# Output projection of a hybrid decoder layer by pairs of column blocks, part of it in seven products

## The chip, the cores and the metric

One core of a Trainium2 chip runs the whole layer in one program. The metric is the device time of one execution in microseconds (us). TensorE (PE in the profile) multiplies, VectorE (DVE) and ScalarE (ACT) do the elementwise work, GpSimd (POOL) and SyncE (SP) mostly issue transfers.

## The reference

Batch 1, 256 tokens, width 2048, everything in float32. The part that matters:

```python
mixed = sigmoid(g_a) * y_a + sigmoid(g_b) * y_b          # (256, 2048); y_a: gated DeltaNet, y_b: pooling mixer
x = x + einsum('bsd,de->bse', mixed, w_out)              # the output projection, w_out (2048, 2048)
h = rmsnorm(x, norm_ffn_w)
gate, up = split(einsum('bsd,df->bsf', h, w_up), 2)      # the up projection, w_up (2048, 11264)
```

`g_a` is the last of the input products (`w_in`, 2048 x 14368) that are made for each of four groups of 512 features (four heads).

## The kernel before, in words

*Numbers.* Each float32 operand is split into a high part (rounded to the reduced format of the fast matmul) and a low part (the rest), and a product is the sum of three matmuls: high by high, low by high, high by low. A weight tile is 256 rows by 512 columns, held as 128 partitions x 2 x 512. ScalarE makes its high part (`whi`, line 317), VectorE its low part (`wlo`, line 328). There are three buffers of each, and `weights()` asks for the split of the tile two ahead (`AHEAD`). Raw tiles come over SP's queue in the order of the list `srcs`, into four buffers (`load_part`, line 223).

*A product.* `gemm_a` makes 256 tokens x 512 columns: for each weight tile, two blocks of 128 features, two halves of the tokens, three matmuls (lines 365 to 367), so twelve matmuls of 128x512. After each six it calls `side()`, which advances a generator of other work by one step.

*The order of groups.* For g = 0 to 3 the input products go k, q, v, p, g_b, z and g_a (eight tiles each, and two of the pooling weights). The delta rule `gdn(g, ...)` is such a generator. For g = 3 its last part runs behind: it waits until `ending` is set, which is done before the last two tiles of the g_a product, and its matmuls (lines 1011 to 1078) are put between those of g_a and of the output projection, one step for each `side()`. The order on TensorE is there fixed as written (`fixed_order`); elsewhere a planner orders every engine by a model of the time, earlier instructions of the program first. After the generator come `gated` (lines 1211, 1215) and, four steps later, `mixed`, which transposes the last group's result and writes its halves `mhi[3]`, `mlo[3]` (lines 1229, 1230).

*The output projection.* Column blocks c = 0 to 3 of 512. Since `mhi[3]` comes late, `early` first makes the tiles 0 to 5 of blocks 0 and 1, with the generator beside them (24 calls of `side()`); then `drain()` ends what is left of it, the mixer's memory pool is closed and that of the feed-forward part (`fp`) is opened in its place. Then tiles 6 and 7 of blocks 0 and 1, and blocks 2 and 3 whole. After each block VectorE adds it to the residual `xts[c]` (line 1270; x came over POOL's queue, line 1258), ScalarE squares it (line 1277), and TensorE transposes it, ScalarE and VectorE scaling and splitting the four rows (lines 1288, 1294, 1295) into `fhl`, the input of the up projection.

*Seven products.* The up projection and the down projection are in part made by the Strassen-Winograd form: two blocks of features by two halves of tokens, and two by two weight tiles (`b11, b12, b21, b22`), need seven products of 256 features by 128 tokens by 512 columns, six matmuls each (`high_first`), in place of eight. Their weights are `b11`, `b21`, `b22` ("11", "21", "22") and four sums T1 to T4, which VectorE makes in place (`up_sum`, line 244) from the loaded quarters (`quad_load`, line 237). T3 and T4 are made from T2 and T2 from T1. The sums of the inputs are made by `four_sums`. In the up projection these products stand between full tiles. A bank is copied (ScalarE) after product 11 and two sums (VectorE, lines 1433 and 1454) are put into other banks before 21 and after T3.

Of the kernel before, what the change touches and what calls it, by code (L numbers as in the profile page):

```python
# [35 lines left out]
def kernel(  # L36
# [40 lines left out]
    def cols(w, base, nk):  # L77
        return [w[c * 256 : (c + 1) * 256, base : base + 512].rearrange("(k p) f -> p k f", p=P)
                for c in range(nk // 2)]

    srcs = []
    for g in range(4):
        for base in (C_K, C_Q, C_V, C_P, C_GB):
            srcs += cols(w_in[0], base + 512 * g, KD)
            if g == 0 and base == C_K:
                srcs += [w_in[0, c * 1024 : (c + 1) * 1024, C_B : C_B + P].rearrange("(k p) f -> p k f", p=P)
                         for c in range(2)]
        parts = [cols(pool_w[0, g], 0, 4), cols(w_in[0], C_Z + 512 * g, KD)]
        for part in parts if g == 3 else parts[::-1]:
            srcs += part  # L90
        srcs += cols(w_in[0], C_GA + 512 * g, KD)
    outw = [cols(w_out[0], 512 * c, KD) for c in range(4)]

    srcs += outw[0][:6] + outw[1][:6] + outw[0][6:] + outw[1][6:] + outw[2] + outw[3]
    NUP = DFF // 512
    TWO = (1, 2, 3, 4, 5, 6, 7, 9)
    chunks_of = [()] + [(1, 0) if c in TWO else (0,) for c in range(1, NUP)]
    UP_PARTS = ("T1", "11", "T2", "21", "T3", "22", "T4")
    up_w = [(cols(w_up[0], 512 * c, KD), cols(w_up[0], DFF + 512 * c, KD)) for c in range(NUP)]
    up_steps = []  # L100
    TAIL = 3
    for c in range(NUP):
# [129 lines left out]
    def quad_load(c, n):  # L232

        ch, i = n // 4, (1, 0, 3, 2)[n % 4]
        up_quarters[c, ch, i] = fp.tile([P, 2, 512], F32, tag=UP_HOMES[1 - c % 2][ch][i], name=nm("quad"))
        with tc.issue_after(last_load[0]):
            last_load[0] = nc.sync.dma_start(up_quarters[c, ch, i], up_w[c][i % 2][2 * ch + i // 2]).ins

    def up_sum(c, what, ch):
        b11, b12, b21, b22 = (up_quarters.get((c, ch, i)) for i in range(4))  # L240
# [53 lines left out]
    def begin(n):  # L294
        while len(made) < min(len(srcs), n):
            load(len(made) + 1)
            raw = loads[len(made)]
            if isinstance(raw, tuple):
                raw, plus, minus = raw
                nc.vector.tensor_tensor(raw, plus, minus, op=ALU.subtract)  # L300
            src = srcs[len(made)]
            shape = list(raw.shape)
            keep = kept.get(len(made))
            behind_conv = ExitStack()
            for ins in last_conv.values():
# [11 lines left out]
            last_cast[0] = nc.scalar.copy(hi, raw).ins  # L317
            if shape[1] == 8:
                lo = None
                nc.vector.tensor_tensor(hi[:, :, 32:64], raw[:, :, 0:32], hi[:, :, 0:32].bitcast(F32),  # L320
                                        op=ALU.subtract)
            else:
                if fourth:
                    lo = fp.tile(shape, F32R, tag="s", name=nm("wlo"))
                else:
                    lo = wpool.tile(shape, F32R, tag="wlo", name=nm("wlo")) if keep is None else \
                        mtile(4 + keep, shape, F32R, nm("klo"))
                last_split[0] = nc.vector.tensor_tensor(lo, raw, hi.bitcast(F32), op=ALU.subtract).ins  # L328
# [3 lines left out]
            made.append((hi, lo))  # L332
            for more in sums_behind.get(len(made) - 1, ()):
# [19 lines left out]

    def gemm_a(lh, ll, nk, steps=None, ps=None):

        ps = pm() if ps is None else ps
        for c in range(nk // 2) if steps is None else steps:
            if c == 1:
                while later:
                    later.pop(0)()  # L360
# [1 line left out]
            for kk in range(2):  # L362
                k = 2 * c + kk
                for t in range(2):
                    mm(ps[:, t, :], lh(k, t), hi[:, kk, :], start=(k == 0), stop=False)  # L365
                    mm(ps[:, t, :], ll(k, t), hi[:, kk, :], start=False, stop=False)  # L366
                    mm(ps[:, t, :], lh(k, t), lo[:, kk, :], start=False, stop=(k == nk - 1))  # L367
                side()
        return ps

    banks = [0]

# [487 lines left out]
    def gdn(g, kq, vt, conv, res):  # L860
# [231 lines left out]
        yield  # L1092
        res.append((po, ro))

    for g in range(4):
        kq = mp.tile([P, 4, 2, S], F32, tag="kq", bufs=1, name=nm("kq"))
        for kind, dst in ((1, kq[:, :, 0, :]), (0, kq[:, :, 1, :])):
            ps = ps_k0 if kind == 1 and g == 0 else gemm_a(xh, xl, KD)
            e = evict(ps)
            convs.append(conv_silu(e, kind, g, dst))  # L1100
            if g:
                later.append(lambda conv=convs[-1]: sum(1 for _ in conv))
            elif kind:
# [152 lines left out]
    def residual(c):  # L1256
        cs = slice(c * 512, (c + 1) * 512)
        return nc.gpsimd.dma_start(xts[c], x[0, :, cs].rearrange("(t p) d -> p t d", p=P)).ins

    residual(0)  # L1260
    residual(1)
    fhl = features("fhl")
    ssq4 = cpool.tile([P, 2, 4], F32, tag="ssq4", name="ssq4b")
    for c in range(4):
        if c < 2:
            ps = gemm_a(at(mhi), at(mlo), KD, range(6, 8), early[c])
        else:
            ps = gemm_a(at(mhi), at(mlo), KD)
        xs = xts[c]
        nc.vector.tensor_tensor(xs, xs, ps, op=ALU.add)  # L1270
        written = nc.gpsimd.dma_start(xt_d[:, :, c * 512 : (c + 1) * 512], xs).ins
# [38 lines left out]
    def four_sums(a11, a12, a21, a22, hi, lo):  # L1310

        s = fp.tile([P, 4, S], F32, tag="s", name=nm("sums"))
        s1, s2, s3, s4 = (s[:, n].rearrange("p (k s) -> p k s", k=2) for n in range(4))
        nc.vector.tensor_tensor(s1, a21, a22, op=ALU.add)
        nc.vector.tensor_tensor(s2, s1, a11, op=ALU.subtract)
        nc.vector.tensor_tensor(s3, a11, a21, op=ALU.subtract)
        nc.vector.tensor_tensor(s4, a12, s2, op=ALU.subtract)
# [4 lines left out]
    def by_halves(h):  # L1322
        return [h[:, 2 * j : 2 * j + 2, t * P : (t + 1) * P] for t in range(2) for j in range(2)]

    y_d = {c: dpool.tile([P, 4, S], F32, tag=f"y{c}", bufs=1, name=f"y{c}") for c in (7, 8, 9)}

# [81 lines left out]

    def fl(k, t):
        return both(fhl, k)[:, 1, t * P : (t + 1) * P]  # L1410

    def high_first(uses, w, first=False):

        for n in range(2):
            for kk in range(2):
                for ps, high, low in uses:
                    for lhs in (high, low) if n == 0 else (high,):
                        mm(ps, lhs(kk), w[n][:, kk], start=(first and n == 0 and kk == 0 and lhs is high), stop=False,  # L1418
                           skip_group_check=True)

    def up_product(c, what, ch):

# [315 lines left out]
```

## Time and profile before

| | |
|---|---|
| median of three runs | 1537.29 us (1536.48 to 1538.0) |
| span of the profiled execution | 1536.8 us |
| TensorE busy | 1524.3 us (99%) |
| VectorE busy | 1268.3 us (83%) |
| ScalarE busy | 853.1 us (56%) |
| split of a weight tile on VectorE (line 328, raw tiles) | 418 times, 1220 ns |
| cast of a weight tile on ScalarE (line 317, raw tiles) | 420 times, 1052 ns |
| output projection on TensorE | from 719.43 us to the last of its products at 818.9 us |

The profiled execution's span agrees with the median of the runs to 0.5 us. A busy share is the time in which the engine has an instruction in flight; matmuls overlap, so the time of a stretch is read from the starts of its instructions. A row of the timeline has start and duration in us, engine, line, operation, output<-inputs, shape and count, and in brackets the idle time before it with what ended it. Rows with a count of more than one are merged.

### The profile page before, as it was taken

How to read it: one execution, taken by the hardware profiler on the slowest of the kernel's cores; microseconds unless marked ns; L12 is line 12 of the kernel's file. 1: busy time of each engine (PE TensorE's matmuls, PEld its weight loads, DVE VectorE, ACT ScalarE, POOL GpSimd, SP SyncE). 2: the span in 40 equal slices, each digit the busy share in tenths (PEclk: the TensorE clock that was granted, in tenths of full speed). 3: DMA queues.
4: the chain of work that ended last, by engine and by line, in shares of the span. 5: the costliest groups of instructions: out<-in, count | busy, mean ns of one | idle time of the engine just before them, and what ended most of it. 6: DMA issues, size and time to landing. Idle time of an engine off the chain costs nothing. (4 is left out here: it accounts for less than half of the span.)

```text
span 1536.8 us, 20233 instructions
## 1 busy us (share of the span) xinstructions
PE 1524.3 (99%) x7290; PEld 1255.4 (82%) x7290; DVE 1268.3 (83%) x1793; ACT 853.1 (56%) x1070; POOL 80.9 (5%) x105
## 2 busy tenths in 40 slices
PE   9999999999999999999999999999999999999997
PEld 8887888787878888788888888788888888888876
DVE  6788859896589858887567899999999886889896
ACT  6455446454455445454455666666666665555553
POOL 1010002000100000000000000000000011010200
PEclk9999999999999999999999999999999999999999
DMA  8776757776576766776588556656457478566662
GB/s 276 209 229 198 203 165 207 218 216 185 148 250 201 208 169 194 231 195 186 171 263 305 179 178 219 219 206 206 154 165 243 127 238 266 172 223 207 235 201 98
DMA packets 166515, 313.62 MB, mean 204 GB/s; under 512 B 19554, under 2 KB 23426, under 8 KB 166286
## 3 DMA queue, kind: packets, MB, share of 16 engines
q1 hardware_dynamic: 157280, 283.17, 59.2%
q0 software_dynamic: 7344, 27.27, 5.5%
q10 hardware_dynamic: 1790, 1.89, 0.4%
q8 instruction: 57, 0.93, 0.3%
q14 instruction: 44, 0.36, 0.1%
HBM read 303.33 MB, written 8.95 MB: 203 GB/s over the span
## 5 line engine op out<-in xcount | busy, mean ns | idle before, releaser
L317 ACT CAST whi<-raw 128x1024 fp32r<-128x1024 f32 x420 | 441.2, 1052 | 427.1 <-PE psm L366 270.0
L328 DVE TENSOR_TENSOR wlo<-raw,whi 128x1024 fp32r<-128x1024 f32 x418 | 507.7, 1220 | 146.0 <-ACT whi L317 140.2
L317 ACT CAST whi<-quad 128x1024 fp32r<-128x1024 f32 x182 | 190.5, 1053 | 136.8 <-PE psg L1418 43.5
L328 DVE TENSOR_TENSOR wlo<-quad,whi 128x1024 fp32r<-128x1024 f32 x182 | 220.0, 1219 | 30.0 <-ACT whi L317 29.4
L367 PE MATMUL psm<-wlo,xhl 128*128 128x512 f32 x432 | 169.5, 393 | 1.3 <-DVE wlo L328 1.2
L365 PE MATMUL psm<-whi,xhl 128*128 128x512 f32 x432 | 169.0, 391 | 0.0
L366 PE MATMUL psm<-whi,xhl 128*128 128x512 f32 x432 | 168.6, 390 | 0.0
L1418 PE MATMUL psg<-whi,fhl 128*128 128x512 f32 x504 | 127.2, 390 | 0.0
L1418 PEld LDWEIGHTS psg<-whi,fhl 128*128 128x128 f32 x504 | 94.5, 188 | 19.6
L367 PEld LDWEIGHTS psm<-wlo,xhl 128*128 128x128 f32 x432 | 81.1, 188 | 18.8 <-DVE wlo L328 2.2
L366 PEld LDWEIGHTS psm<-whi,xhl 128*128 128x128 f32 x432 | 81.1, 188 | 16.8
L365 PEld LDWEIGHTS psm<-whi,xhl 128*128 128x128 f32 x432 | 81.1, 188 | 16.7
L244 DVE TENSOR_TENSOR quad<-quad,quad 128x1024 f32<-128x1024 f32 x72 | 87.6, 1216 | 0.0
L1418 PE MATMUL psg<-wlo,fhl 128*128 128x512 f32 x252 | 69.9, 389 | 0.0
L1418 PE MATMUL psg<-whi,ups 128*128 128x512 f32 x216 | 58.9, 394 | 0.0
L1418 PEld LDWEIGHTS psg<-wlo,fhl 128*128 128x128 f32 x252 | 47.3, 188 | 9.9
L1403 PE MATMUL psm<-whi,hhi 128*128 128x512 f32 (+1 forms) x140 | 54.5, 389 | 0.1
L1403 PE MATMUL psm<-whi,hlo 128*128 128x512 f32 (+1 forms) x140 | 54.1, 386 | 0.0
L1403 PE MATMUL psm<-wlo,hhi 128*128 128x512 f32 (+1 forms) x140 | 54.0, 387 | 0.0
L365 PE MATMUL psm<-whi,mhi 128*128 128x512 f32 x128 | 50.8, 397 | 0.0
L367 PE MATMUL psm<-wlo,mhi 128*128 128x512 f32 x128 | 50.0, 390 | 0.0
L366 PE MATMUL psm<-whi,mlo 128*128 128x512 f32 x128 | 49.9, 390 | 0.0
(435 smaller groups left out, 2953.7 us busy)
## 6 DMA issues: line engine op xcount, KB each, us to landing
raw<-in_w_in_dram SPq DMA_DIRECT2D x224, 512.0 KB, 4.3
raw<-in_w_up_dram SPq DMA_DIRECT2D x104, 512.0 KB, 4.8
quad<-in_w_up_dram SPq DMA_DIRECT2D x72, 512.0 KB, 5.0
raw<-in_w_down_dram SPq DMA_DIRECT2D x56, 512.0 KB, 5.1
raw<-in_w_out_dram SPq DMA_DIRECT2D x32, 512.0 KB, 4.2
quad<-in_w_down_dram POOLq DMA_DIRECT2D x32, 512.0 KB, 5.3
mv<-vrow SPq DMA_DIRECT2D x12, 512.0 KB, 4.8
taps<-in_conv_qkv_w_dram SPq DMA_DIRECT2D x16, 256.0 KB, 6.6
```

What stands on the lines that cost most here:

```text
L244: nc.vector.tensor_tensor(out_, plus_, minus_, op=ALU.subtract)
L317: last_cast[0] = nc.scalar.copy(hi, raw).ins
L328: last_split[0] = nc.vector.tensor_tensor(lo, raw, hi.bitcast(F32), op=ALU.subtract).ins
L365: mm(ps[:, t, :], lh(k, t), hi[:, kk, :], start=(k == 0), stop=False)
L366: mm(ps[:, t, :], ll(k, t), hi[:, kk, :], start=False, stop=False)
L367: mm(ps[:, t, :], lh(k, t), lo[:, kk, :], start=False, stop=(k == nk - 1))
L1403: mm(ps[:, cs], lhs(kk), part_[:, kk, cs], start=(first and kk == 0 and n == 0), stop=(last and kk == 1 and n == 2), skip_group_check=shared)
L1418: mm(ps, lhs(kk), w[n][:, kk], start=(first and n == 0 and kk == 0 and lhs is high), stop=False, skip_group_check=True)
```

## The change

The output projection is made by pairs of column blocks (0 and 1, then 2 and 3). For the first four feature blocks (tiles 0 and 1 of each column block of the pair, which need only `mhi[0]`, `mlo[0]`) the eight products of the two by two form become seven (`pair_product`), one after the other, with no full tile between them; their results lie in the banks in which the remaining tiles (2 to 7) are then added by `gemm_a`. In the first pair `side()` is called after products 1, 3, 5 and 6 (counted from 0), and then after each six matmuls of the tiles 2 to 5 of both blocks. The sums of the input (`out_sums`) are made during the value product of group 3 and split into `osum` during the last g_a product. So that `osum` has a place (the memory of the last four feature blocks of the input), the g_a product of group 3 takes the feature blocks in another order (`GA_LAST`). The quarters of the weights go to memory that other tiles have left (`out_home`), the last two of the second pair to the feed-forward pool.

```diff
+    GA_LAST = (6, 7, 0, 1, 2, 3, 4, 5)
-        srcs += cols(w_in[0], C_GA + 512 * g, KD)
+        ga = cols(w_in[0], C_GA + 512 * g, KD)
+        srcs += ga if g < 3 else [ga[c] for c in GA_LAST]
-    srcs += outw[0][:6] + outw[1][:6] + outw[0][6:] + outw[1][6:] + outw[2] + outw[3]
+    out_pairs = [("out", p) for p in range(2)]
+    srcs += [("up", out_pairs[0], what, 0) for what in UP_PARTS] + outw[0][2:6] + outw[1][2:6]
+    srcs += outw[0][6:] + outw[1][6:]
+    srcs += [("up", out_pairs[1], what, 0) for what in UP_PARTS] + outw[2][2:] + outw[3][2:]
...
+    quads_behind = {}
+    for pair in out_pairs:
+        n = first_part(pair)
+        sums_behind[n - 1] = [(pair, "T1", 0)]
+        for i in range(4 if pair == out_pairs[0] else 2):
+            quads_behind.setdefault(n - 6 + i, []).append((pair, i))
...
+    def out_home(pair, i):
+        if pair == out_pairs[0]:
+            if i < 2:
+                if not halves_kq:
+                    halves_kq.append(mp.tile([P, 2, 2, 512], F32, tag="kq", bufs=1, name=nm("quads")))
+                return halves_kq[0][:, i]
+            return mp.tile([P, 2, 512], F32, tag=("ev", "crow")[i - 2], name=nm("quad"),
+                           **(dict(bufs=1) if i == 2 else {}))
+        if i < 2:
+            return big.tile([P, 2, 512], F32, tag=("x2a", "x2b")[i], name=nm("quad"))
+        return fp.tile([P, 2, 512], F32, tag=("hhi4", "hlo4")[i - 2], name=nm("quad"))
...
+    def pair_product(bank, what, tokens, sums):
+        a, b = bank["ps"]
+        if what in ("11", "21", "T4"):
+            j, t = {"11": (0, 0), "21": (1, 0), "T4": (1, 1)}[what]
+            high, low = (lambda kk, f=f: f(2 * j + kk, t) for f in tokens)
+        else:
+            n = {"T1": 0, "T2": 1, "T3": 2, "22": 3}[what]
+            high, low = (lambda kk, s=s: s[:, n, kk * P : (kk + 1) * P] for s in sums)
+        if what == "21":
+            nc.vector.tensor_tensor(b[:, 0], a[:, 1], bank["own"], op=ALU.add)
+        w = weights()
+        ps = {"T1": a[:, 0], "21": a[:, 0], "22": b[:, 0]}.get(what, a[:, 1])
+        high_first([(ps, high, low)], w, what in ("T1", "11"))
+        if what == "T1":
+            bank["own"] = cpool.tile([P, 512], F32, tag="sqj", name=nm("own"))
+            nc.scalar.copy(bank["own"], a[:, 0])
+        elif what == "11":
+            nc.scalar.copy(a[:, 0], a[:, 1])
+        elif what == "T3":
+            nc.vector.tensor_tensor(b[:, 1], a[:, 1], bank["own"], op=ALU.add)
...
+    def out_sums():
+        h = mp.tile([P, 4, S], F32, tag="mv", name=nm("whole"))
+        nc.vector.tensor_tensor(h, mhi[0].bitcast(F32), mlo[0].bitcast(F32), op=ALU.add)
+        out_s.append(mp.tile([P, 4, S], F32, tag="pu", name=nm("sums")))
+        sums_into(out_s[0], *by_halves(h))
...
-            ps = gemm_a(xh, xl, KD, range(6))
+            ps = gemm_a(xh, xl, KD, GA_LAST[:6])
             ending.append(True)
-            ps = gemm_a(xh, xl, KD, range(6, 8), ps)
+            osum = big.tile([P, 2, 4, S], F32R, tag="x3", name="osum")
+            nc.scalar.copy(osum[:, 0], out_s[0])
+            with tc.issue_after(last_split[0]):
+                nc.vector.tensor_tensor(osum[:, 1], out_s[0], osum[:, 0].bitcast(F32), op=ALU.subtract)
+            ps = gemm_a(xh, xl, KD, GA_LAST[6:], ps)
...
-    early = [gemm_a(at(mhi), at(mlo), KD, range(n)) for n in (6, 6)]
+    def out_pair(sides=()):
+        bank = {"ps": (pm(), pm())}
+        pair = out_pairs[1 if made_pairs else 0]
+        made_pairs.append(bank["ps"])
+        for n, what in enumerate(UP_PARTS):
+            pair_product(bank, what, (at(mhi), at(mlo)), (osum[:, 0], osum[:, 1]))
+            if n in sides:
+                side()
+        return bank["ps"]
+
+    made_pairs = []
+    early = [gemm_a(at(mhi), at(mlo), KD, range(2, 6), ps) for ps in out_pair((1, 3, 5, 6))]
     drain()
...
+    for i in (2, 3):
+        quad_load(out_pairs[1], i)
     residual(0)
...
-            ps = gemm_a(at(mhi), at(mlo), KD)
+            if c == 2:
+                early += out_pair()
+            ps = gemm_a(at(mhi), at(mlo), KD, range(2, 8), early[c])
```

`UP_PARTS` is ("T1", "11", "T2", "21", "T3", "22", "T4"), the order of the seven products. `sums_into` holds the four sums that `four_sums` made in place; `high_first` and `by_halves` are moved up unchanged.

More of the change, by code (lines that the diff above doesn't have):

```diff
@@ L79, in cols @@
                 for c in range(nk // 2)]
+    GA_LAST = (6, 7, 0, 1, 2, 3, 4, 5)
+    UP_PARTS = ("T1", "11", "T2", "21", "T3", "22", "T4")
     srcs = []
@@ L97 @@
     chunks_of = [()] + [(1, 0) if c in TWO else (0,) for c in range(1, NUP)]
-    UP_PARTS = ("T1", "11", "T2", "21", "T3", "22", "T4")
-    up_w = [(cols(w_up[0], 512 * c, KD), cols(w_up[0], DFF + 512 * c, KD)) for c in range(NUP)]
+    up_w = {c: (cols(w_up[0], 512 * c, KD), cols(w_up[0], DFF + 512 * c, KD)) for c in range(NUP)}
+    up_w |= {pair: outw[2 * p : 2 * p + 2] for p, pair in enumerate(out_pairs)}
     up_steps = []
@@ L234, in quad_load @@
         ch, i = n // 4, (1, 0, 3, 2)[n % 4]
-        up_quarters[c, ch, i] = fp.tile([P, 2, 512], F32, tag=UP_HOMES[1 - c % 2][ch][i], name=nm("quad"))
+        if c in out_pairs:
+            home = out_home(c, i)
+        else:
+            home = fp.tile([P, 2, 512], F32, tag=UP_HOMES[1 - c % 2][ch][i], name=nm("quad"))
+        up_quarters[c, ch, i] = home
         with tc.issue_after(last_load[0]):
             last_load[0] = nc.sync.dma_start(up_quarters[c, ch, i], up_w[c][i % 2][2 * ch + i // 2]).ins
+    halves_kq = []
+    def out_home(pair, i):
[9 more added lines that the diff above has]
+        return fp.tile([P, 2, 512], F32, tag=("hhi4", "hlo4")[i - 2], name=nm("quad"))
     def up_sum(c, what, ch):
@@ L332, in begin @@
             made.append((hi, lo))
+            for more in quads_behind.get(len(made) - 1, ()):
+                quad_load(*more)
             for more in sums_behind.get(len(made) - 1, ()):
@@ L354, in gemm_a @@
     def gemm_a(lh, ll, nk, steps=None, ps=None):
+        steps = range(nk // 2) if steps is None else steps
+        first = 2 * steps[0] if ps is None else None
+        last = nk - 1 if ps is not None else 2 * steps[-1] + 1
+        seeded = dict(skip_group_check=ps is not None)
         ps = pm() if ps is None else ps
-        for c in range(nk // 2) if steps is None else steps:
+        for c in steps:
             if c == 1:
@@ L364, in gemm_a, with high_first @@
                 for t in range(2):
-                    mm(ps[:, t, :], lh(k, t), hi[:, kk, :], start=(k == 0), stop=False)
-                    mm(ps[:, t, :], ll(k, t), hi[:, kk, :], start=False, stop=False)
-                    mm(ps[:, t, :], lh(k, t), lo[:, kk, :], start=False, stop=(k == nk - 1))
+                    mm(ps[:, t, :], lh(k, t), hi[:, kk, :], start=(k == first), stop=False, **seeded)
+                    mm(ps[:, t, :], ll(k, t), hi[:, kk, :], start=False, stop=False, **seeded)
+                    mm(ps[:, t, :], lh(k, t), lo[:, kk, :], start=False, stop=(k == last), **seeded)
                 side()
         return ps
+    def pair_product(bank, what, tokens, sums):
[3 more added lines that the diff above has]
+            high, low = (lambda kk, f=f: f(2 * j + kk, t) for f in tokens)
+        else:
+            n = {"T1": 0, "T2": 1, "T3": 2, "22": 3}[what]
[12 more added lines that the diff above has]
+            nc.vector.tensor_tensor(b[:, 1], a[:, 1], bank["own"], op=ALU.add)
+    def high_first(uses, w, first=False):
+        for n in range(2):
+            for kk in range(2):
+                for ps, high, low in uses:
+                    for lhs in (high, low) if n == 0 else (high,):
+                        mm(ps, lhs(kk), w[n][:, kk], start=(first and n == 0 and kk == 0 and lhs is high), stop=False,
+                           skip_group_check=True)
     banks = [0]
@@ L1093, in gdn, with by_halves, sums_into @@
         res.append((po, ro))
+    def by_halves(h):
+        return [h[:, 2 * j : 2 * j + 2, t * P : (t + 1) * P] for t in range(2) for j in range(2)]
+    def sums_into(s, a11, a12, a21, a22):
+        s1, s2, s3, s4 = (s[:, n].rearrange("p (k s) -> p k s", k=2) for n in range(4))
+        nc.vector.tensor_tensor(s1, a21, a22, op=ALU.add)
+        nc.vector.tensor_tensor(s2, s1, a11, op=ALU.subtract)
+        nc.vector.tensor_tensor(s3, a11, a21, op=ALU.subtract)
+        nc.vector.tensor_tensor(s4, a12, s2, op=ALU.subtract)
+    out_s = []
+    def out_sums():
[3 more added lines that the diff above has]
+        sums_into(out_s[0], *by_halves(h))
     for g in range(4):
@@ L1100 @@
             convs.append(conv_silu(e, kind, g, dst))
+            if g == 3 and kind == 0:
+                later.append(out_sums)
             if g:
@@ L1312, in four_sums @@
         s = fp.tile([P, 4, S], F32, tag="s", name=nm("sums"))
[L1313 to L1317, printed above, removed]
+        sums_into(s, a11, a12, a21, a22)
         nc.scalar.copy(hi, s)
@@ L1320, in four_sums @@
         return hi, lo
-    def by_halves(h):
-        return [h[:, 2 * j : 2 * j + 2, t * P : (t + 1) * P] for t in range(2) for j in range(2)]
     y_d = {c: dpool.tile([P, 4, S], F32, tag=f"y{c}", bufs=1, name=f"y{c}") for c in (7, 8, 9)}
@@ L1410, in fl @@
         return both(fhl, k)[:, 1, t * P : (t + 1) * P]
[L1412 to L1419, printed above, removed]
     def up_product(c, what, ch):
```

## The prediction

> **What bounds the kernel now.** I read the page first, then the waits of TensorE, then the timeline of TensorE and VectorE around the output projection (us from the span's start).
>
> ```profile
> span 1536.8 us, 20233 instructions
> PE 1524.3 (99%) x7290; PEld 1255.4 (82%) x7290; DVE 1268.3 (83%) x1793; ACT 853.1 (56%) x1070; POOL 80.9 (5%) x105
> ...
> PE psm L367 <- DVE wlo L328: 1.5, 2, 1.2
> ```
>
> TensorE (PE) works all the time; its longest wait for a weight split adds up to 1.5 us. So the time is TensorE's instruction stream, and a change helps by what it removes from that stream and hurts by each wait it puts in. What is one matmul worth?
>
> ```profile
> 702.04 0.39 PE L365 MATMUL psm<-whi,xhl1a 128*128 128x512 f32 x1
> ...
> 704.76 0.39 PE L365 MATMUL psm<-whi,xhl1b 128*128 128x512 f32 x1
> ```
>
> Twelve matmuls, those of one weight tile, start between these two rows: 2.72 us a tile, 0.227 us a matmul. The 0.39 us in the duration column overlaps the next one and is no price. Beside it the VectorE (DVE), which splits each weight tile into a high and a low half and, in the seven-product form, makes the weight sums:
>
> ```profile
> 863.22 1.22 DVE L244 TENSOR_TENSOR quad<-quad,quad 128x1024 f32<-128x1024 f32 x1
> 864.36 1.22 DVE L328 TENSOR_TENSOR wlo<-quad,whi 128x1024 fp32r<-128x1024 f32 x1
> ...
> L1433 DVE TENSOR_TENSOR psg<-psg,own x10: 686/690/693, 873.2 to 1256.8; 128x512 f32<-128x512 f32 x10
> L1447 ACT COPY own<-psm x10: 574/580/582, 857.4 to 1245.1; 128x512 f32<-128x512 f32 x10
> ```
>
> Back to back, a split or a sum costs VectorE 1.135 us (start to start), a 128x512 addition on PSUM 0.69, and a copy of that size on ScalarE (ACT) 0.58. Today a tile gives TensorE 2.72 us of work for 1.135 us of VectorE. A product of the new form is six matmuls, 1.36 us of TensorE, for 1.135 us of split, and four of seven also need a sum of 1.135. That ratio decides the change. The two places where the pairs go (the third row is the value product of group 3), and in the last two rows the weight splits alone:
>
> ```profile
> core 0: us, PE busy (x) PEld busy (x) DVE busy (x) ACT busy (x) POOL busy (x), PEclk, DMA share, GB/s
> 719.43:728.94 9.51, 9.51 (x82) 7.54 (x81) 8.16 (x14) 5.13 (x7) 0.00 (x0) 1.00 0.57 187
> 772.88:784.00 11.12, 11.12 (x59) 9.44 (x58) 8.29 (x13) 8.50 (x16) 1.41 (x2) 1.00 0.99 322
> 600.00:620.00 20.00, 20.00 (x101) 16.82 (x100) 19.96 (x36) 13.61 (x21) 0.00 (x0) 1.00 0.79 239
> ...
> 719.43:728.94 9.51, 3.33 (x3) 1.00 0.57 187
> 772.88:784.00 11.12, 3.78 (x4) 1.00 0.99 322
> ```
>
> In the first 9.51 us of the projection (as long as 42 matmuls) VectorE is already busy for 8.16 us, 3.33 of it splits and 4.83 the end of the delta-rule work of group 3. Where column block 2 begins it has 8.29 us, 3.78 of splits and 4.51 of residual work.
>
> **The change part by part.**
>
> *Matmuls.* Per pair, four tiles (48 matmuls) become seven products (42). Two pairs: 12 x 0.227 = 2.7 us off TensorE. This is all that the change can gain. By the duration column it would be 12 x 0.39 = 4.7; the pitch decides.
>
> *Pair 0 (column blocks 0 and 1).* Its first two products are split before the last tile of the input product ends. The third, T2, needs a weight buffer (three of them) which that tile holds to its end:
>
> ```profile
> 719.40 1.05 ACT L317 CAST whi<-raw 128x1024 fp32r<-128x1024 f32 x1 [0.72 <-PE psm L366]
> ...
> 720.49 1.23 DVE L328 TENSOR_TENSOR wlo<-raw,whi 128x1024 fp32r<-128x1024 f32 x1 [0.96 <-ACT whi L317]
> 721.78 1.22 DVE L1204 SCALAR_TENSOR_TENSOR sz<-gate,sz 128x1024 f32<-128x1024 f32 x1
> 723.04 1.26 DVE L1031 TENSOR_SCALAR T<-psg 32x128 f32<-32x128 f32 x4
> ...
> 726.71 1.30 DVE L1032 STREAM_TRANSPOSE TT<-T 32x128 f32<-32x128 f32 x4
> ```
>
> So VectorE can begin T2's split about 1.1 us after that tile's end, as in row 720.49, which waits for the cast of 719.40. From there to the last product T4 it has five splits (T2, 21, T3, 22, T4) and the sums T3 and T4, which hang on T2: 7 x 1.135 = 7.95; two additions 1.38; and the 4.8 us that were there anyway (lines 1204, 1206 which follows it, 1031, 1032 and the rest). Together 14.1 us. The end comes at 1.1 + 14.1 + 1.36 = 16.6 us, where 42 matmuls and one small group (0.6) take 10.1: a wait of 6.4. If that delta-rule work all slips behind the pair, 1.1 + 9.3 + 1.36 = 11.8 against 9.5: 2.3. I take 5.5, nearer the high end, since lines 1204 and 1206 stand earlier in program order and are ready within 2.3 us. Inside this lies the wait of T2 for ScalarE's copy of the bank that it adds to (0.58 and a ScalarE queue that holds a gate of two activations): about 1 us, no addition to the sum.
>
> *Pair 1.* The same 9.3 us and the 4.5 us of residual work, one start of 1.1 and one last product: 16.3 against 11.1 us, a wait of 5.2; with the residual work behind the pair 2.3. I take 4.2, between them: the four-row evictions may fall behind T4, the addition of block 1 cannot.
>
> *Side calls.* Before, the delta-rule generator is advanced 24 times in the 144 matmuls of `early` (after each six); the last transposes (`mixed`) come at the 23rd. Now there are 4 + 16 = 20 calls, so they come out of `drain()`, after the last matmul.
>
> ```profile
> 747.02 1.05 PE L1076 MATMUL psg<-w,ga 128*128 128x128 f32 x8
> ...
> 756.69 0.87 DVE L1215 SCALAR_TENSOR_TENSOR sz<-sz,ro,yb 128x128 f32<-128x128 f32 x3
> ...
> 759.72 1.03 PE L410 MATMUL psg<-ident,sz 128*128 128x128 f32 x8
> 760.51 0.47 PE L365 MATMUL psm<-whi,mhi 128*128 128x512 f32 x1
> ...
> 760.97 1.29 DVE L1230 TENSOR_TENSOR mlo<-psg,mhi 128x512 fp32r<-128x512 f32 x2 [0.34 <-ACT mhi L1229]
> ```
>
> The state's output product (15th call) starts at 747.02 and the gated rows it leads to end at 757.56, 10.5 us later, through ScalarE, VectorE and POOL. Behind the 15th call there were eight half tiles (10.9 us) ahead of the transposes; now five (6.8 us, and 1.7 for the product): TensorE waits 10.5 - 8.5 = 2.0. Then it transposes for 0.8 us and needs the first low half of block 3, ready (760.97 + 0.68) 1.9 us after the transposes' start; the six matmuls from 760.51 on that covered this are gone: 1.1 more. Sum 3.1; ends 0.5 (the chain runs faster with fewer splits between) and 5. I take 3.
>
> *Loads.* Bytes are the same. The last two quarters of pair 1 go to memory that the mixer's pool holds, and stand on SP ahead of the last two raw tiles of block 1.
>
> ```profile
> 761.47 1.64 POOL L1258 DMA_DIRECT2D xt<-in_x_dram  x2 [6.41 <-ACT mhi L1229]
> ...
> xt<-in_x_dram POOLq DMA_DIRECT2D x4, 512.0 KB, 7.0
> ```
>
> The rows of x that wait for that same memory go out at 761.47, after block 3's transposes, and take 7.0 us to land. A raw tile behind the quarters would land about 7 us after that, plus 2.2 us of cast and split, against 5.4 us of cover (two tiles): up to 3.8 us; nothing if the planner, which orders the queue by when it expects each transfer to be ready, issues it first. That is the likelier, so 0.5. The first pair's quarters go where the gating work has long ended; hidden by the eight tiles of the input product.
>
> *Sums of the mixed rows.* One 1.135 us addition and four half-size ones (0.69) on VectorE, 3.9 us, made in the value product, where VectorE is busy 19.96 of 20.00 us; splits there run up to two tiles ahead, so 0; ends 0 and 1.5. The split of the sums (one cast, one 1.135) sits in the last input tiles. Reordering the feature blocks only renames which tile comes when: 0.
>
> *Sum.* -2.7 + 5.5 + 4.2 + 3.0 + 0.5 = +10.5 us: 1547.3 against the span of 1536.8, 1547.8 against the median of 1537.29, which lies 0.5 above the profiled span.
>
> **The rivals.** A change within 3 us (0.2%) is about what a measurement here can't tell from none.
>
> *Hidden after all (other side).* If VectorE's chain from T2 on fits in the six products ahead of T4 (8.2 us), TensorE never waits, and the time is 1537.3 - 2.7 = 1534.6, or 1534 to 1540 with a wait left at the drain. For it:
>
> ```profile
> 878.01 1.07 PE L1418 MATMUL psg<-whi,ups 128*128 128x512 f32 x4
> ...
> 879.37 1.07 PE L1418 MATMUL psg<-whi,ups 128*128 128x512 f32 x4
> ```
>
> Products run at 1.36 us each without a gap in the up projection (879.37 - 878.01). Against it: there the sums were made before, between full tiles, two feature chunks take turns on one bank, and a fourth buffer is kept; here the splits and sums alone need 9.3 us. It decides at 8.2 us of VectorE work. Chance 0.16.
>
> *Only the drain costs.* VectorE's other work slips out of both pairs (2.3 each) and the drain costs 3: 1537.3 - 2.7 + 2.3 + 2.3 + 3 = 1542. This is the low part of my forecast, chance 0.25.
>
> *The clock falls.* The granted clock is 1.00 in all windows above, in which TensorE never rests. A pair full of waits of 1 to 3 us may lose it; at half the clock 42 matmuls cost 9.5 us more, 1557. Chance 0.04: the waits of a pair fall into three or four pieces with matmuls between. [...] No row of this trace shows such a fall.
>
> **How the numbers follow.** Forecast (VectorE bounds both pairs, the drain waits), 0.55, 1543 to 1554; only the drain 0.25; clock 0.04; hidden 0.16, of which up to 0.03 faster by over 0.2% (full success, 2.7 us, does not reach 3.1). So slower 0.82, same 0.15, faster 0.03. The range, 1538 to 1555, leaves out the better half of the hidden case and the clock case.
>
> **What would show it.** In the changed kernel: twelve matmuls fewer; TensorE idle before the 128x512 products T2, T3 and T4 with VectorE (the addition or the split) as releaser, several us in each pair; VectorE without idle time through both pairs; the transposes of group 3 right after the last early tile, with idle time on both sides of them. Wrong if the pair's 42 matmuls span under 11 us, or if the evictions of residual rows move out of pair 1.

## The result, and the profile after

| | before | after |
|---|---|---|
| median of the runs (us) | 1537.57 (1536.48 to 1538.0) | 1562.33 (1561.28 to 1564.33) |
| ratio, 95% interval | | 1.0162 (1.015 to 1.0174) |
| profiled span (us) | 1536.8 | 1562.6 |
| matmuls | 7290 | 7278 |

The change costs 24.8 us. The forecast was 10.5 with 1538 to 1555 as its range: the sign is right, the size is not. The page of the changed kernel:

```profile
span 1562.6 us, 20241 instructions
...
PE 1534.8 (98%) x7278; PEld 1258.1 (81%) x7278; DVE 1289.3 (83%) x1817; ACT 861.9 (55%) x1081; POOL 79.8 (5%) x105
...
PEclk9999999999999999998989999999999999999999
```

PEclk is the clock that TensorE was granted, one digit for each fortieth of the span, in tenths of full clock (9 is 90% or more). Twelve matmuls fewer, yet TensorE is busy for longer (1534.8 against 1524.3), and two of the 40 slices have lost clock. Both slices are those of the pairs. TensorE's waits in the changed kernel (total us, times, longest us; line 435 is the products' matmul, 423 ScalarE's copy of T1's bank, 425 its copy behind 11, 417 and 427 VectorE's additions ahead of 21 and behind T3):

```profile
PE psm L435 <- ACT own L423: 5.4, 2, 3.1
PE psm L435 <- DVE psm L427: 4.1, 2, 3.2
...
PE psm L435 <- DVE psm L417: 1.7, 2, 0.9
PE psm L435 <- ACT psm L425: 1.6, 2, 0.8
PE psg L477 <- DVE sz L1307: 0.7, 1, 0.7
PE psm L402 <- DVE mlo L1322: 0.5, 1, 0.5
```

The first four lines, 12.8 us, are two waits each: one in each pair. No product waits for a weight split. The timeline of TensorE shows where they stand; a product is a row with osum (a sum of blocks: T1, T2, T3, 22) or mhi (a block itself: 11, 21, T4), in the order T1, 11, T2, 21, T3, 22, T4:

```profile
722.81 1.09 PE L435 MATMUL psm<-whi,osum 128*128 128x512 f32 x4
...
726.70 0.58 PE L435 MATMUL psm<-whi,mhi 128*128 128x512 f32 x1 [2.34 <-ACT own L423]
...
730.22 2.08 PE L435 MATMUL psm<-whi,osum 128*128 128x512 f32 x4 [0.81 <-ACT psm L425]
...
734.01 0.50 PE L435 MATMUL psm<-whi,mhi 128*128 128x512 f32 x1 [0.86 <-DVE psm L417]
...
741.04 2.04 PE L435 MATMUL psm<-whi,osum 128*128 128x512 f32 x4 [3.18 <-DVE psm L427]
...
745.26 0.39 PE L401 MATMUL psm<-whi,mhi 128*128 128x512 f32 x1
```

```profile
790.23 1.17 PE L435 MATMUL psm<-whi,osum 128*128 128x512 f32 x4
...
796.46 0.80 PE L435 MATMUL psm<-whi,mhi 128*128 128x512 f32 x1 [3.10 <-ACT own L423]
...
810.12 1.16 PE L435 MATMUL psm<-whi,osum 128*128 128x512 f32 x4 [0.88 <-DVE psm L427]
...
812.93 0.39 PE L401 MATMUL psm<-whi,mhi 128*128 128x512 f32 x1
```

Pair 0 takes 745.26 - 722.81 = 22.45 us and pair 1 812.93 - 790.23 = 22.70. Without a wait and at the pitch of 0.227 they would take 10.1 (42 matmuls and a small group of the solve) and 10.3 (42 and one group of transposes): 12.3 and 12.4 us too long. Both pairs in one view:

```profile
core 0: us, PE busy (x) PEld busy (x) DVE busy (x) ACT busy (x) POOL busy (x), PEclk, DMA share, GB/s
722.81:745.26 22.45, 15.25 (x75) 10.48 (x74) 17.60 (x26) 9.60 (x12) 0.00 (x0) 0.77 0.07 23
790.23:812.93 22.70, 16.66 (x53) 11.73 (x52) 16.19 (x21) 12.94 (x22) 1.41 (x2) 0.70 0.28 82
```

No engine is busy all the time. TensorE, VectorE and ScalarE wait for each other in turn, and TensorE's granted clock (the number after POOL's) is at 0.77 and 0.70. That is the picture of a chain through three engines, and not of a VectorE that is full, which the prediction had.

Look at which products wait. T2 needs ScalarE's copy behind 11 by its data, since it adds to the bank that the copy reads. But 11 goes to the second bank of a two-bank accumulator and waits for the copy *out of the first*; 21 adds to the first bank of accumulator a and waits for VectorE's addition that only reads a's second; 22 adds to b's first bank and waits for the addition that writes b's second. None of these three needs what it waits for. The program's accumulators are tiles of [128, 2, 512], two banks each, and the dependency holds for the tile.

### The profile page after: what moved, and what is told of

Its sections match the earlier page's. It is cut to its first block, busy times and chain, and to the rows that moved or that the text cites. A ratio compares the mean times of both kernels' runs of the same rounds, so it can differ in the third digit from the quotient of the medians.

```text
span 1562.6 us, 20241 instructions
## 1 busy us (share of the span) xinstructions
PE 1534.8 (98%) x7278; PEld 1258.1 (81%) x7278; DVE 1289.3 (83%) x1817; ACT 861.9 (55%) x1081; POOL 79.8 (5%) x105
## 5 line engine op out<-in xcount | busy, mean ns | idle before, releaser
L347 ACT CAST whi<-raw 128x1024 fp32r<-128x1024 f32 x412 | 432.4, 1052 | 419.7 <-PE psm L402 263.0
L358 DVE TENSOR_TENSOR wlo<-raw,whi 128x1024 fp32r<-128x1024 f32 x410 | 497.5, 1219 | 144.5 <-ACT whi L347 139.6
L347 ACT CAST whi<-quad 128x1024 fp32r<-128x1024 f32 x191 | 199.3, 1053 | 148.1 <-PE psg L435 53.4
L358 DVE TENSOR_TENSOR wlo<-quad,whi 128x1024 fp32r<-128x1024 f32 x191 | 230.8, 1218 | 32.5 <-ACT whi L347 31.7
L403 PEld LDWEIGHTS psm<-wlo,xhl 128*128 128x128 f32 x432 | 81.1, 188 | 19.2 <-DVE wlo L358 2.8
L274 DVE TENSOR_TENSOR quad<-quad,quad 128x1024 f32<-128x1024 f32 x76 | 92.4, 1216 | 0.0
L1503 PE MATMUL psg<-whi,hhi 128*128 128x512 f32 (+1 forms) x120 | 46.6, 389 | 0.4 <-ACT whi L347 0.4
L1503 PE MATMUL psg<-whi,hlo 128*128 128x512 f32 (+1 forms) x120 | 46.3, 386 | 0.0
L435 PEld LDWEIGHTS psg<-whi,ups 128*128 128x128 f32 x216 | 39.8, 188 | 8.0
```

Of the source, the lines that this page charges most:

```text
L274: nc.vector.tensor_tensor(out_, plus_, minus_, op=ALU.subtract)
L1503: mm(ps[:, cs], lhs(kk), part_[:, kk, cs], start=(first and kk == 0 and n == 0), stop=(last and kk == 1 and n == 2), skip_group_check=shared)
```

## The experiments

**Theory A:** the missing 14 us are dependencies of whole accumulator tiles, which put each product behind a copy or an addition of the other bank. **Theory B:** they are the clock, which falls in the gaps. **Theory C:** VectorE's work, as predicted, only more of it.

**One-bank tiles.** All two-bank accumulators become two tiles of one bank; nothing else differs but that operations over both banks are split in two. The same was done to the kernel before as a control.

```
-        return psm.tile([P, 2, 512], F32, tag="m", name=nm("psm"))
+        return Banks(lambda n: psm.tile([P, 512], F32, tag=f"m{n}", name=nm("psm")))
```

> The changed kernel, with each pair of PSUM banks of the big products made two tiles of one bank in place of one tile of two (three whole-tile operations on VectorE become two halves each, some 0.15 us more apiece). Theory A (a product waits for the copy or addition of the other bank, because both banks are one tile): the waits of product 11 for the copy of T1 (2.3 and 3.1 us), of 21 for the first addition (0.9 and 0.9) and of 22 for the second (3.2 and 0.9) go; TensorE rests less, the clock stays at 1.00, and the time falls from 1562 to about 1543 to 1550, what VectorE's chain and the drain leave. Theory B (VectorE's and ScalarE's queues are what is late, the tile does not matter): other waits take their place, 1558 to 1564.

> The kernel before with the same tiles of one bank: the control of the run above. Both theories: TensorE had no waits there, so 1537 to 1540.

Measured: the changed kernel 1550.22, ratio 1.0077 (1.006 to 1.0094); the control 1536.89, 0.9996 (0.9986 to 1.0005). The first is at the edge of theory A's 1543 to 1550 and far from theory B's 1558. So one-bank tiles take 12 of the 24.8 us away, and nothing where no product waits; the 12 hold the waits and what clock they had cost. What is left, +12.2, is near the 10.5 that the prediction had counted as all. The waits in it (lines 434 and 436 are now the copies, 428 and 438 the additions), the start of T4 in pair 0, pair 0 as a window, and ScalarE's timeline ahead of the longest wait, in pair 1:

```profile
PE psm L446 <- ACT psm L436: 6.4, 2, 5.3
PE psm L446 <- DVE psm L438: 2.4, 1, 2.4
...
PE psm L446 <- DVE psm L428: 0.6, 1, 0.6
PE psm L446 <- DVE wlo L369: 0.6, 1, 0.6
...
734.75 0.77 PE L446 MATMUL psm<-whi,mhi 128*128 128x512 f32 x1 [2.39 <-DVE psm L438]
...
720.22:737.45 17.23, 12.65 (x76) 8.99 (x74) 16.79 (x26) 9.58 (x12) 0.00 (x0) 0.92 0.02 8
```

```profile
787.81 0.47 ACT L1416 ACTIVATE fhl1b<-psg,vec 128x256 fp32r<-128x256 f32 x1
788.17 0.64 ACT L1399 ACTIVATE sqj<-xt 128x512 f32<-128x512 f32 x1
...
788.78 1.05 ACT L358 CAST whi<-quad 128x1024 fp32r<-128x1024 f32 x1
...
790.08 0.60 ACT L434 COPY own<-psm 128x512 f32<-128x512 f32 x1
790.55 0.51 ACT L1416 ACTIVATE fhl<-psg,vec 128x256 fp32r<-128x256 f32 x1
790.92 0.63 ACT L436 COPY psm<-psm 128x512 f32<-128x512 f32 x1
...
791.60 2.07 PE L446 MATMUL psm<-whi,osum 128*128 128x512 f32 x4 [5.34 <-ACT psm L436]
```

11 and 22 no longer wait, and 21 only for its split (0.6 us). What waits in pair 0 is T2 for the copy (1.0), T3 for the first addition (0.6) and T4 for the second (2.39): each adds to the bank that the copy or addition reads. Pair 0 is now near the predicted case: VectorE is busy for 16.79 of 17.23 us, 7.1 us over the 10.1 (5.5 forecast). Not all of that is VectorE: the clock is at 0.92, and T4's six matmuls take 737.45 - 734.75 = 2.70 us, where 1.36 is the pitch, so about 1.3 of the 7.1 is lost clock. Pair 1 is still not the predicted case: TensorE stands for 5.34 us before T2 for a copy of 0.63 us that ScalarE reaches only behind squares, row evictions and a cast. The prediction gave this wait "about 1 us, no addition".

**The clock.** Spare matmuls, 44 in all, into a bank that nobody reads, in the places of the gaps; once with the order left to the planner in pair 1, once with it fixed.

```
+        spare = pg()
...
+            for _ in range((9, 3, 3, 0, 9, 0, 0)[n]):      # pair 1: (11, 3, 3, 0, 3, 0, 0)
+                mm(spare, mhi[0][:, 0, 0:P], mhi[1][:, 0:2, :], start=True, stop=True)
```

> The changed kernel with matmuls into a spare bank that nobody reads, put where TensorE waited: behind T1 (9 in the first pair, 11 in the second), 11 (3), T2 (3) and T3 (9 and 3); 0.227 us each, 44 in all. Theory of the clock (some 9 us of the loss are matmuls at half the granted clock, because TensorE rested): the granted clock stays 1.00 through both pairs and the time falls to about 1552 to 1555, the waits being the same. Rival (the slow matmuls are slow for their operands or banks, or the loss is the waits alone): the clock or the matmuls stay as they are, 1562 or up to 10 us more for the added matmuls.

> As the filled kernel before it, with the order of TensorE fixed in the second pair too, so that the 20 added matmuls there stand behind T1, 11, T2 and T3 and are not bunched behind 11. Theory of the clock: the granted clock is 1.00 through both pairs, each pair takes 19.5 to 20.5 us in place of 22.5, and the time is 1556 to 1558. Rival (half the clock is no cost of its own, only the waits are): each pair takes 22 us or more, 1561 or more.

Measured: 1561.13, 1.0155 (1.014 to 1.017), and 1561.47, 1.0155 (1.0141 to 1.0168). Both times theory B's expectation missed (1552 to 1555, then 1556 to 1558). In pair 1 the test spoilt itself both times: in the first the planner put 20 spare matmuls in one heap behind 11, in the second the spare matmuls waited 3.6 us for their own bank. Pair 0 is clean in both. It takes 19.91 us in the first (720.50 to 740.41) and, at full clock all through, 20.00 in the second, against 22.45:

```profile
721.60:741.60 20.00, 17.04 (x99) 12.59 (x99) 17.40 (x26) 9.61 (x12) 0.00 (x0) 1.00 0.03 7
```

So of the 12.3 us in pair 0 the clock is 2.4, and 9.9 stay with the clock at 1.00: theory B alone is refuted there. In this pair slow matmuls mostly fill what would else be a wait.

**Parts of the change.** Everything but the pairs (order of feature blocks, the sums of the mixed rows); and the first pair alone, blocks 2 and 3 as before:

```
-    for pair in out_pairs:
+    for pair in out_pairs[2:]:
-    early = [gemm_a(at(mhi), at(mlo), KD, range(2, 6), ps) for ps in out_pair((1, 3, 5, 6))]
+    early = [gemm_a(at(mhi), at(mlo), KD, range(n)) for n in (6, 6)]
```
```
-    out_pairs = [("out", p) for p in range(2)]
+    out_pairs = [("out", 0)]
-            ps = gemm_a(at(mhi), at(mlo), KD, range(2, 8), early[c])
+            ps = gemm_a(at(mhi), at(mlo), KD)
```

> All that the change does beside the pairs: the other order of the last input product, the sums of the mixed rows and their split, with the output projection as before and no use of the sums. If these parts cost nothing, 1536 to 1539. If the sums hurt in the value product, where VectorE was busy all the time, 1539 to 1541.

> The changed kernel with the first pair in seven products and the second as before. If the two pairs cost alike and add (their spans were 22.5 and 22.7 us), half of the loss goes with the second: its waits and slow matmuls, 12 us, against the 1.4 us that its six matmuls fewer had saved: 1550 to 1553. If the loss is mostly in the first pair and the drain: 1556 or more.

Measured: without pairs 1538.82, 1.0009 (1.0 to 1.0019), some 0.8 us; pair 0 alone 1551.68, 1.0098 (1.0083 to 1.0114), 14.5 of the 24.8 us. Both first expectations held. The second run also gives, unasked, a pair 0 with the same instructions and mostly full clock. Its row of product 11 and its window, and two short windows of it and of the changed kernel, the gap ahead of 11 and what follows it:

```profile
724.33 0.50 PE L435 MATMUL psm<-whi,mhi 128*128 128x512 f32 x1 [2.34 <-ACT own L423]
...
720.45:742.11 21.66, 13.03 (x76) 9.16 (x75) 17.69 (x26) 9.61 (x12) 0.00 (x0) 0.92 0.08 24
...
721.99:724.33 2.34, 0.00 (x1) 0.00 (x0) 2.34 (x3) 2.29 (x3) 0.00 (x0) 1.00 0.00 0
724.33:728.00 3.67, 2.46 (x10) 1.72 (x10) 3.67 (x4) 1.53 (x2) 0.00 (x0) 1.00 0.01 2
```

```profile
724.36:726.70 2.34, 0.01 (x1) 0.01 (x1) 2.34 (x3) 2.28 (x3) 0.00 (x0) 1.00 0.00 0
726.70:730.00 3.30, 2.71 (x6) 1.61 (x6) 3.30 (x4) 1.36 (x2) 0.00 (x0) 0.54 0.01 2
```

The same gap of 2.34 us behind the same matmuls: once the clock halves behind it, once it does not. And the pair takes 21.66 us with a mean clock of 0.92, 22.45 with 0.77: 0.8 us between them.

**More side calls.** All seven products of pair 0 advance the solve (four did), and two of its steps take two calls (three): its end comes five calls earlier.

```
-        yield from step(3)
+        yield from step(2)      # at two places
...
-    early = [gemm_a(at(mhi), at(mlo), KD, range(2, 6), ps) for ps in out_pair((1, 3, 5, 6))]
+    early = [gemm_a(at(mhi), at(mlo), KD, range(2, 6), ps) for ps in out_pair(range(7))]
```

> The changed kernel with a side call after every product of the first pair (23 calls in place of 20) and two waits of the delta-rule generator one call shorter, so that the last transposes come one tile ahead of the end of the early tiles and not out of the drain. Theory (the drain costs some 2 us there: 0.7 before and 0.7 after the transposes' first, and the half rate of the transposes): 1559 to 1560.5. Rival (the generator's work, drawn into the pair, makes its waits longer by as much): 1562 or more.

Measured: 1556.34, 1.0122 (1.0108 to 1.0135), 19.2 us over the kernel before: 5.6 less than the change, where about 2 to 3 were expected (1559 to 1560.5, missed). The half rate of the transposes in that sum is not shown: seven of them take 1.11 us in the changed kernel, at a clock of 1.00, and eight take 1.03 here. The drain's part is as expected; in the changed kernel it was these waits (0.72, 0.15, 0.52, together 1.4), and here the transposes come without one (the second fence):

```profile
776.35 1.11 PE L477 MATMUL psg<-ident,sz 128*128 128x128 f32 x7 [0.72 <-DVE sz L1307]
777.62 0.73 PE L401 MATMUL psm<-whi,mhi 128*128 128x512 f32 x2 [0.15 <-ACT mhi L1321]
...
778.87 0.50 PE L402 MATMUL psm<-whi,mlo 128*128 128x512 f32 x1 [0.52 <-DVE mlo L1322]
```

```profile
770.37 1.03 PE L477 MATMUL psg<-ident,sz 128*128 128x128 f32 x8
```

The rest was not aimed at. The start of T1 in pair 0 of this run, and its pair 1 from T1 to the end of T4:

```profile
723.09 1.09 PE L435 MATMUL psm<-whi,osum 128*128 128x512 f32 x4
...
785.68:804.39 18.71, 11.89 (x53) 8.52 (x52) 16.15 (x21) 12.66 (x22) 1.41 (x2) 1.00 0.37 113
```

The same 53 matmuls and transposes, clock 1.00 and not 0.70, and 18.71 us, not 22.70: 4.0 less. TensorE's waits in it are no shorter (6.8 us in all, 6.0 in the changed kernel), so it is the matmuls that are faster: in pair 1 the lost clock did count. The parts don't add up to the 5.6, though. From T1 of pair 0 to T1 of pair 1 this run takes 785.68 - 723.09 = 62.59 us, the changed kernel 790.23 - 722.81 = 67.42, so 4.8 less, of which the drain's waits are 1.4; the other 3.4 lie in pair 0 and the tiles behind it, where the steps of the solve stand in other places. Together that is 8.8; the two profiled spans differ by 7.5 and the medians by about 6. VectorE's waits in pair 1 of the changed kernel say why the clock counted there: it stood for 3.1 us ahead of its additions, for products that ran at half the clock (0.50 from 796.46 to 808.38 us).

```profile
DVE psm L417 <- PE psm L435: 2.2, 1, 2.2
DVE psm L427 <- PE psm L435: 0.9, 1, 0.9
```

In pair 1 of this run it waits for no product, and in pair 0 of the changed kernel it did so for 0.9 us only.

**Cover by order.** If a pair is a chain T1, copy, 11, copy, T2, addition, 21, then tiles of other column blocks between its products should hide it. One-bank tiles; T1, 11 and T2 of pair 0 between the last three tiles of the last input product; T1, 11, T2 and 21 of pair 1 between tiles 6 and 7 of blocks 0 and 1; side calls as in the run above.

```
+            for n in range(3):
+                pair_product(bank0, UP_PARTS[n], tokens0, (osum[:, 0], osum[:, 1]))
+                if n == 1:
+                    ending.append(True)
+                ps = gemm_a(xh, xl, KD, GA_LAST[5 + n : 6 + n], ps)
...
+            for i in range(2):
+                ps = gemm_a(at(mhi), at(mlo), KD, range(6 + i, 7 + i), early[c])
+                out_part(bank1, UP_PARTS[2 * c + i])
```

> Seven products kept in both pairs, but spread: T1, 11 and T2 of the first pair between the last three tiles of the input product, T1, 11, T2 and 21 of the second between the four tiles 6 and 7 of blocks 0 and 1 (its results in the small PSUM banks), one-bank tiles, a side call after each product that is left, and the two shorter waits. Theory (the loss is products back to back, with a queue to wait for after each): the waits fall to 0 to 5 us in all, the clock stays, and the 2.7 us of matmuls are had in part: 1535 to 1540. Rival (VectorE lacks the time even so): 1542 or more.

Measured: 1537.02, 0.9998 (0.9989 to 1.0007). The result of this kernel leaves out part of the second pair's additions. The next run, in which nothing is left out, has the same number of instructions on each engine (7278 matmuls, 1829 on VectorE, 1081 on ScalarE). It moves the second accumulator of that pair from the small banks to those of the big products, and the one beside it also puts four tiles of block 1 ahead of T4 of pair 0:

```
-    bank1 = {"ps": tuple(Banks(lambda n: pg()) for _ in range(2))}
+    bank1 = {"ps": (Banks(lambda n: pg()), pm())}
```
```
+    early = [None, gemm_a(at(mhi), at(mlo), KD, range(2, 6), bank0["ps"][1])]
+    out_part(bank0, "T4")
```

> [...] The instructions on TensorE are the same in number and order. If the time of a pair is what TensorE waits for and nothing else: 1536 to 1539, like the run before (1537.0), since the saved 2.7 us of matmuls are eaten by the 1.6 us wait of T4 for the second addition and 1.2 us of a wait in the solve. If pair 1's accumulator now has to wait for block 0 and 1 to be added to the rows, 21 of pair 1 waits about 2 us more: 1539 to 1541.

> As the run beside it, and in pair 0 the four early tiles of block 1 (12 matmuls each, which use bank sums that are complete after 22) are put ahead of T4, so that the second addition has some 10 us of cover and not 1.1 us. If T4's wait of 1.57 us was on the path: 1.5 to 2 us less than the run beside it, 1534.5 to 1537, and no wait of T4 in the trace. If the end is set by the side chain and its two waits on VectorE anyway (the additions, the splits and the solve share VectorE, which has no gap there): the same time, with the wait moved to the next transposes of the drain.

Measured: 1537.79, 1.0004 (0.9994 to 1.0013), and 1537.48, 0.9998 (0.999 to 1.0007). So the same products with the same 12 matmuls fewer cost nothing that these runs can tell from none once they are spread: the 24.8 us were order and tiles, the earlier side calls among them. A spread with two-bank tiles was not run, so what each of the three gives in this form is not told apart. They do not gain either; the second of these runs missed the 1534.5 to 1537 of its first expectation. TensorE's waits at the projection in the second of these kernels (line 1094 is the solve's first product, 417 an early tile):

```profile
PE psg L1094 <- DVE T L1070: 2.0, 2, 1.7
...
PE psm L417 <- DVE psm L443: 0.6, 1, 0.6
PE psg L451 <- DVE psm L443: 0.2, 1, 0.2
PE psg L1130 <- DVE TT L1115: 0.2, 1, 0.2
```

T4's wait of 1.57 us is gone as asked, and 0.6 of it has come back at the tile put there; the solve waits 2.0 us for VectorE's transposes, which stand between splits. Together 3.0 us, about the 2.7 that the matmuls saved; the kernel before shows no wait of TensorE between 700 and 830 us. The next run starts the solve one call later.

```
-                if n == 1:
+                if n == 2:
                     ending.append(True)
```

> As the kernel with the four tiles ahead of T4, and the last solve begins one call (one tile) later: in that kernel its products at 720 to 722 us wait 2.0 us for VectorE's transposes of its matrix, which stand between splits. If this wait is lost time: 1.5 to 2 us less than that kernel's 1537.5, 1535 to 1536.5, a ratio near 0.999, and no wait of these products in the trace. If the drain at the end of the early tiles becomes late by the one call (in that kernel its transposes come at 762 us with tiles to run until 772): no change, a wait for the gated rows or the cast before the last tiles. If 12 matmuls fewer are not 2.7 us in this place but are given back at VectorE's other work, the time stays within 0.1% of before.

Measured: 1541.32, 1.0022 (1.0013 to 1.0031), some 3 us over the kernel before. None of the expected times came. The mechanism is the second of the expectations: the solve's wait is gone, and the transposes of the drain wait 3.2 us for the gated rows. TensorE's waits at the projection are 4.9 us in all, 1.9 more than in the run above, which explains about half of the 3.8 us between the two.

```profile
PE psg L493 <- DVE sz L1332: 3.2, 2, 2.4
...
PE psm L451 <- DVE psm L433: 0.6, 1, 0.6
```

No kernel tried here beats the one before.

## Why the prediction was wrong

*Matmuls, -2.7: right in number.* 12 fewer (7278), at an unchanged pitch of 0.227 us where nothing waits; no run shows the 2.7 us by themselves.

*Pair 0, 5.5, and pair 1, 4.2: the step that failed, 12.3 and 12.4 measured.* Three things were missing in it. First, the prediction let a product depend on the banks that it uses; the program's tiles are two banks, and 11, 21 and 22 each stood behind a copy or an addition of the bank beside theirs. One-bank tiles gave 12 us back, the clock that went with these waits included. Second, the sum had VectorE's queue in it and none for ScalarE: a copy of 0.6 us was taken as "about 1 us, no addition", but in pair 1 it stands behind other evictions, 3.10 us ahead of 11 in the changed kernel and 5.34 ahead of T2 with one-bank tiles. "The four-row evictions may fall behind T4" was the wrong way round. (The 11.1 us that pair 1 was compared with also hold two groups of transposes; one stood in it, hence the 10.3 above.) Third, the clock, below. Where the first two are mostly out of the way, as in pair 0 with one-bank tiles, VectorE's chain is what was described: the waits stand before T2, T3 and T4, and the pair is 7.1 us too long for the 5.5 (worked out as 6.4), some 1.3 of it clock.

*The clock, a rival with chance 0.04: too low, and for a wrong reason.* "The waits of a pair fall into three or four pieces" is true, and the clock halved all the same, behind gaps of 2.34 to 3.18 us (0.77 and 0.70 over the pairs). The rival's price was 9.5 us for 42 matmuls at half the clock, which are those of one pair; the two pairs have 84. The windows in the prediction have a clock of 1.00 alone, so the half was assumed there; the changed kernel shows 0.50. For a pair the price was too high: the clock was at half for a part of it only (0.50 from 796.46 to 808.38 us in pair 1, and in pair 0 from 728 to 733 and from 741.04 to 744), and in pair 0 slow matmuls filled time in which TensorE would have waited (22.45 us with a mean clock of 0.77, 21.66 with 0.92). By the run with spare matmuls and the one with more side calls the clock's part is about 2.4 us in pair 0 and 4.0 in pair 1; these are comparisons with other kernels, in which the order of VectorE's work is a little different too, so they are estimates.

*Drain, 3.0: 1.4 in waits;* the mechanism was right, and the last run shows 3.2 us of such waits when the solve comes one call later. *Loads, 0.5: 0;* no wait of TensorE at the projection has a transfer as its releaser. *Sums and order, 0 (0 to 1.5): 0.8,* in an interval from 0 to 2.9.

*The sum by these: -2.7 + 12.3 + 12.4 + 1.4 + 0.8 = 24.2 against 24.8.* The parts come from one execution, the slowest of four, whose span is 25.8 us over the one before; 3.4 of that lies ahead of pair 0 (T1 starts at 722.81, the projection began at 719.43), so the sum is good to an us or two. That the forecast had the sign right says little for its mechanism: the tiles and ScalarE's queue were not in it. Of what the prediction named as signs, the twelve matmuls and the idle time at the transposes came true; the idle time before T2, T3 and T4 with VectorE as releaser did not. 11, 21 and 22 waited, and T2 for ScalarE's copy (0.8 us in each pair). "VectorE without idle time through both pairs" was false (17.60 of 22.45 and 16.19 of 22.70 us), and that line of the windows alone tells the case from the one forecast.

## What to carry to other kernels

Before a sum is made for products that pass results between banks, write down for each the tile that it touches, not the bank: copies and additions on a neighbour in the same tile were on the path here, for about 12 us. A chain of product, copy, product, addition needs other matmuls between its links, and in it every engine has a queue whose order is a term of its own, the engine that seems to have time included: TensorE stood here for 5.34 us for a copy of 0.63. A form that removes one part in eight of the matmuls can be hidden by spreading it, but it must find room on the other engines; here, at the best, the 2.7 us saved came back as waits of 3.0.

## What the runs showed of the hardware that was not expected

In the changed kernel the granted clock was 0.54 in the 3.3 us behind a TensorE gap of 2.34 us, 0.50 in the 11.9 us behind one of 3.10 and 0.50 in the 3.0 us behind one of 3.18. The same gap of 2.34 us behind the same instructions left it at 1.00 in another run, and in pair 1 of the run with more side calls, which has a gap of 2.48, it was 1.00 all through. In pair 0 of that run a gap of 1.72 us came ahead of a fall: the first four matmuls behind it started 0.23 to 0.33 us apart, the two from 728.00 us on took 0.77 us together where the last two of T1 took 0.61, and from 729.48 us on, behind a further gap of 0.72, the clock was 0.50.

```profile
726.97 0.50 PE L435 MATMUL psm<-whi,mhi 128*128 128x512 f32 x1 [1.72 <-ACT own L423]
...
729.48:732.34 2.86, 2.86 (x7) 1.82 (x7) 2.77 (x5) 1.79 (x2) 0.00 (x0) 0.50 0.00 0
```

So the length of a gap alone does not tell here whether the clock falls. What does, and whether the 32 small matmuls of 32x32 just ahead of the gap of 1.72 us (0.69 us) bear on it, was not measured.
